# Score products of a block of heads: all over 128 rows first, then those over 64 rows with the halves of the rows in turn

## The chip, the core and the metric

The kernel runs on one core of a Trainium2 chip. The time is device microseconds (us) of one execution, as the median over several runs; lower is better. The program computes a whole small model (two different transformer stacks of two layers each, 256 tokens, model width 1024), with float32 inputs and outputs.

## The reference, cut to what matters

Three attentions of the second stack and one of the first make scores of queries and keys, add a bias or a mask, and take a softmax. Everything else (feed-forward products, experts, a recurrent time mix, output products) is not touched by the change.

```
# second stack, each of 2 layers; D = 64, S = 256
s = jnp.einsum('bhqd,bhkd->bhqk', q, k) * D ** -0.5        # neighbourhood, differential, window attention
p = softmax(s + bias)                                       # over the keys
o = jnp.einsum('bhqk,bkhd->bqhd', p, v)
# first stack, each of 2 layers: the same with a causal mask, for two branches (whole and selected keys)
```

## The kernel before, in words

TensorE (PE) multiplies operands that are split into two float32r parts, a high part and a low part: a product of two float32 numbers then has three terms (high by high, high by low, low by high). A head has 64 columns, so a score product contracts over 64 rows only. The kernel uses this: in a query tile `qs` the high part of a head stands in 64 of the 128 rows and its low part in the other 64; in the key tile `ks` the high part of the keys stands in both halves. One product over all 128 rows (`ks` by `qs`) therefore gives two of the three terms. The third (low part of the keys, `kl`, by the high part of the queries) is a product over the 64 rows of one half. `halves()` names the two halves of the rows: heads of half 0 have their high part in rows 0 to 63, heads of half 1 in rows 64 to 127.

So each head costs two PE products into the same columns of a PSUM bank: one over 128 rows, one over 64 rows. A block of heads takes two banks, one for heads of half 0 (`ps[0]`, `pS[0]`) and one for heads of half 1. `scores()` (lines 1989 to 1998, second stack) makes blocks of eight products, four heads with 256 keys each. `first()` inside `nsa()` (line 1247, first stack) makes blocks of sixteen products for the first 128 tokens (eight heads, 128 keys each) and of eight products for the second 128 tokens (four heads, 256 keys).

A pipeline of steps surrounds this: the scores of a block; then VectorE (DVE) adds the bias and takes the maximum of each head from the bank (line 1361), ScalarE (ACT) takes the exponentials (line 1363); the next block's scores; then PE transposes the first block's probabilities (line 1370) and multiplies them with the values. Between these steps stand pieces of "fill": big weight products (line 426, three passes high-high, low-high, high-low), whose weights arrive by DMA and are split by ACT (line 215) and DVE (line 216). In the first stack the fill also holds the small products of the recurrent mix, over 64 rows and 64 columns (lines 993 to 1150).

The program's order on each engine is fixed when it is built: a scheduler takes instructions out of the written order where its own estimate lets one run earlier. An engine carries out its own list in that order and waits on semaphores for the others.

Of the kernel before, what the change touches and what calls it, by code (L numbers as in the profile page):

```python
# [19 lines left out]
PSUM = bass.MemoryType.PSUM  # L20
# [15 lines left out]
# Big products run on operands that are split exactly into two float32r parts.  # L36
# [12 lines left out]
# A mix's streams are merged by these numbers of steps: time before the units and its fill; time, units and their fill;  # L49
# the last steps of time and the first half of the output product.  # L50
# [85 lines left out]
def _cols(w, at, n, step=512):  # L136
    """Column pieces of w from column at on."""
    return [w[:, c:c + min(step, at + n - c)] for c in range(at, at + n, step)]


def backwards(ap):
    """ap with its last dimension read from the end."""
    dims = [list(d) for d in ap.ap]
    step, n = dims[-1]
    dims[-1] = [-step, n]
    return bass.AP(tensor=ap.tensor, offset=ap.offset + step * (n - 1), ap=dims)


class Feed:
    """The weights in the order of their use, loaded and split into float32r parts ahead of the products."""  # L150
# [12 lines left out]
    def drop(self, phase):  # L163
        """The buffers of a phase go."""
        for kind in range(2):
            self.free[kind][:] = [s for s in self.free[kind] if s[0] != phase]
        assert self.part or not any(s[0] == phase for s in [r[1] for r in self.raws] + [s[1] for s in list(self.subs) + list(self.live)])

    def add(self, phase, srcs, split=True, heads=False):
        """srcs: DRAM [kb*128, n] in the order of their products; heads: columns (g j d) change to (j g d)."""  # L170
# [12 lines left out]
    def load(self):  # L183
        """Starts the next load, if a buffer is free."""
# [41 lines left out]
    def take(self, src):  # L226
        """The next row blocks of src: [(row block, part APs [128, n])]."""
# [6 lines left out]
    def done(self, n=1):  # L234
        """The products with the n oldest row blocks in hand are in the program."""
        for _ in range(n):
            self.free[1].append(self.live.popleft()[1])
# [11 lines left out]
class Operand:  # L249
    """Transposed parts [128, K, 256], put into the program by steps when products are about to need them."""  # L250
# [16 lines left out]
def merge(*streams):  # L267
    """The steps of all, each stream (steps, how many) kept as far along as the others."""
# [16 lines left out]
def weave(main, fill, ratio=1):  # L285
    """The steps of main with ratio steps of fill after each; what is left of fill stays."""
# [8 lines left out]
class Model:  # L295
# [75 lines left out]
    def banks(self, use):  # L371
        """The PSUM banks of a phase, by tag."""
        self.ps_use, self.ps_turn = use, {}
# [9 lines left out]
    def rows_to_columns(self, rows, name):  # L383
        """rows: list of (key, ap [r, 128]); returns a tile [128, R] and the first column of each key."""
# [25 lines left out]
    def put(self, parts, sel, src, scale=None):  # L410
        """parts[sel] = src * scale (scale: per-partition column or None)."""
# [10 lines left out]
    def mm(self, ps, lhs, rhs, start, stop):  # L422
        """lhs, rhs: lists of part APs."""
# [4 lines left out]
    def mul(self, xT, sub, targets, last):  # L428
        """targets: (ps, kind, at, opens, closes); kind 0: token tile at[0] of xT with the columns from at[1] on,
        1: the columns at(part) with xT, transposed; a bank has one that opens and one that closes it."""  # L430
# [10 lines left out]
    def products(self, xT, src, targets, evac, fine=False):  # L441
        """A step for each piece of the weights src; targets() -> as mul takes them; evac() at the end."""
# [17 lines left out]
    def tokens(self, xT, src, evac, banks=("lin", "lin"), tiles=(0, 1), fine=False):  # L460
        """evac(t, ps) with the products [128 tokens, n]."""
# [11 lines left out]
    def linear(self, xT, w, cols, evac, banks=("lin", "lin"), fine=False):  # L473
        """evac(t, c0, n, ps) for each chunk of columns; w: DRAM [K*128, N]."""
# [3 lines left out]
    def transposed(self, parts, src, nb, t, c0=0, k0=0, bank="tr"):  # L478
        """parts[:, k0+b, t*128:] = transposes of the nb column blocks of src [128, nb*128]."""
# [9 lines left out]
    def squares(self, h, ss):  # L489
        """ss[:, :, h] = the sums of squares of half of the columns of x."""  # L490
# [7 lines left out]
    def rstd(self, ss=None):  # L498
        """1/sqrt(mean(x^2) + eps) per token: [128, 2]."""
# [15 lines left out]
    def norm_T(self, gcol, pool=None):  # L515
        """Operand of (x*g) transposed, with rstd [128, 2]."""
# [19 lines left out]
    def start(self, gcol, pool=None):  # L536
        """The next phase's operand, as far as the first half of x's columns makes it."""
# [12 lines left out]
    def ffn(self, pool, xT, w1, w3, w2, done, tiles=(0, 1), hook=None):  # L550
        """Steps; done(t, c0, n, ps) takes the products; hook comes before the last of them."""
# [109 lines left out]
    def small_first(self, pool, l):  # L661
        """Loads the small weights of a layer of the first block."""
# [52 lines left out]
    def rope(self, pool, dst, src, t, heads):  # L715
        """dst, src: [128, heads, 64] of token tile t; the first 16 columns of each head."""
# [81 lines left out]
    def by_halves(self, ops, w, banks, hook=None, order=(0, 1), fine=False):  # L798
        """Steps: x += the products of two operands with the halves of the rows of w."""
# [17 lines left out]
    def mixed(self, l, pool, xT, src, zm, b0):  # L817
        """zm = the products transposed (blocks from b0 on), each token mixed with the one before it."""
# [56 lines left out]
    def head_norm(self, pool, src, eps, name, scratch, eng):  # L875
        """(src - mean) * rsqrt(var + eps) over the last of [128, nt, 4, 64], in scratch[0]."""
# [14 lines left out]
    def rwkv(self, l, pool, sw, zm, out):  # L891
# [5 lines left out]
        # normalised kk  # L897
# [12 lines left out]
        # decay and rates  # L910
# [70 lines left out]
        # products inside chunks of 64 tokens: [A^T | P^T | B^T | Q^T]  # L981
# [19 lines left out]
        # X = (I + A)^-1 by blocks of doubling size  # L1001
# [46 lines left out]
        # operands by token  # L1048
# [19 lines left out]
        # what does not need the state: U = -X B V and G = -X KK  # L1068
# [10 lines left out]
        # from chunk to chunk the state is S' = H^T S + C; the output is R^T S + Y  # L1079
# [38 lines left out]
        # bonus and gate  # L1118
# [39 lines left out]
    def compress(self, l, pool, sw, zk, out):  # L1158
        """out["cmp"]: the compressed keys [128, 32] and values [128, 8, 64], one block a head on the diagonal."""
# [56 lines left out]
    def nsa(self, l, pool, sw, qraw, zk, out):  # L1216
# [6 lines left out]
        # transposes  # L1223
# [23 lines left out]
        def first(t, br, j0):  # L1247
# [8 lines left out]
            for i in range(hb):  # L1256
                for gg, own, _ in self.halves():
                    q = qs[t][:, j0 + i, gg]
                    nc.tensor.matmul(pS[gg][:, i], q, ks[:, br, gg, 0:nk], start=True, stop=False)
                    nc.tensor.matmul(pS[gg][:, i], q[own], kl[own, br, 0:nk], start=False, stop=True)  # L1260
# [30 lines left out]
        # the compressed branch  # L1291
# [42 lines left out]
    def pipeline(self, pool, items, first, last, between=None, tag="tr"):  # L1334
        """Steps; each item's probabilities, their transposes and products, the next item's first ahead of the transposes."""
# [19 lines left out]
    def softmax_exp(self, pool, e, ps, bias, hb, sums, sink=None):  # L1355
        """e = exp(ps + bias - max), sums: its sums over the keys; returns -max; sink: minus what else the maximum takes in."""
# [23 lines left out]
    def ple_products(self, l, pT, pp, fine=False):  # L1380
        """pp [128, 2, 1024] = p @ ple_proj_w, by steps; pT: parts [128, 2, 256] of scratch."""
# [25 lines left out]
    def router(self, l, pool, temp):  # L1407
        """Loads the router's small weights."""
# [13 lines left out]
    def moe(self, l, wr, rb, sums, pp):  # L1422
        """Opens the buffers; yields what begins with the first half of x's columns and what does the rest."""
# [14 lines left out]
    def experts(self, l, pool, fp, ectx, km, gB, wr, rb, sums, pp):  # L1438
# [74 lines left out]
        # the tokens before each in its expert's list, and the lists' lengths  # L1513
# [33 lines left out]
    def dispatch(self, pool, e, off, km, sel, pos, tag, bufs):  # L1547
        """One-hot [128 tokens, 2, 128 slots]: slot off+c of expert e takes the token."""
# [7 lines left out]
    def expert_tokens(self, pool, e, km, sel, pos, gt, hs, got):  # L1556
        """got[e] = an expert's tokens transposed, their weights and 1/rms, and the way back; by steps."""
# [24 lines left out]
    def expert(self, pool, fp, tokens, w1, w3, w2, ahead):  # L1582
        """ahead: steps that make the next expert's tokens."""
# [18 lines left out]
    def expert_over(self, pool, e, km, sel, pos, gt, hs, w1, w3, w2):  # L1602
        """Slots 128 to 255 of an expert."""
# [55 lines left out]
    def row(self, pool, g):  # L1659
        """A vector [1024] in all partitions."""  # L1660
# [4 lines left out]
    def inner_norm(self, gB):  # L1665
        """x normalised, once the operand that is started has all of it; that gets both norms' 1/rms."""
# [8 lines left out]
    def outer_norm(self, pool, gB):  # L1675
        """x normalised, to the output."""
# [93 lines left out]
    def second_setup(self, pool, tp):  # L1770
        """Steps that make the tables of position biases."""
# [33 lines left out]
    def small_second(self, pool, l):  # L1805
        """Loads the small weights of a layer of the second block; w["steps"] makes the neighbourhood's biases."""
# [62 lines left out]
    def along(self, rstd, pool=None, bank="tr"):  # L1869
        """rstd [128, 2] per token -> [128, 256] with the tokens along the columns."""  # L1870
# [11 lines left out]
    def columns(self, xT, src, dst, scale, bank="lin", parts=None):  # L1882
        """dst [128, 256] of each block = the products transposed, by blocks of 128 columns, times rstd and scale;
        parts: what takes dst then."""
# [18 lines left out]
    # Scores are products over 64 rows: the parts of the queries stand above each other, the first part of the keys twice,  # L1903
    # so that one product has two of the three terms.
    def halves(self):
        return [(i, slice(i * 64, i * 64 + 64), slice(64 - i * 64, 128 - i * 64)) for i in range(2)]

    def queries(self, src, dst):
        """dst [128, blocks, 2, 256]: of each half of the rows its first part in place, its second in the other half's."""
# [5 lines left out]
    def keys(self, src, dst, low):  # L1915
        """dst [128, blocks, 2, 256]: of each half of the rows its first part in both halves; low: the second parts."""
# [6 lines left out]
    def attention(self, pool, l, xT, hook):  # L1923
# [14 lines left out]
        def query(c0, n=1):  # L1938
            """Steps and the queries of n times two blocks."""
# [20 lines left out]
        def pairs(q0, k0):  # L1960
            """Steps that make the queries and keys of four blocks, and they by twos."""
# [27 lines left out]
        def scores(qk, t, kb=lambda m: m):  # L1989
            """The scores of two heads of each half of the rows, in a bank each; kb(m): the block of head m's keys."""  # L1990
            qs, ks, kl = qk
            ps = [self.bank("sc").rearrange("p (h k) -> p h k", h=2) for _ in range(2)]
            for m in range(2):
                for i, own, _ in self.halves():
                    q = qs[:, m, i, t * P:(t + 1) * P]
# [233 lines left out]
```

## Time and profile before

| | |
|---|---|
| median of 3 runs | 2845.73 us (2842.85 to 2850.19) |
| span of the profiled execution (first to last instruction) | 2848.1 us |
| instructions in it | 38806 |
| busy share of the span: PE, DVE, ACT, POOL | 98%, 67%, 58%, 5% |
| mean granted PE clock | 0.976 of full speed |

The trace gives the profiled execution no time other than its span, which lies inside the range of the three runs, 2.4 us above their median. Busy time of PE counts an instruction from its start to its modelled end; two that overlap are not counted twice. The mean granted clock is 1 at 2.4 GHz and 0.5 at 1.2 GHz.

### The profile page before, as it was taken

The page shows a single profiled execution, that of the slowest core. Times are in us where ns is not written, and L with a number is a line of the kernel's source. Part 1 is how long each engine was busy: PE and PEld are TensorE (multiplying, and loading weights), DVE is VectorE, ACT ScalarE, POOL GpSimd, SP SyncE. Part 2 cuts the span into 40 slices and gives each one's busy share as a digit, 9 for nine tenths or more (in the row PEclk, how much of TensorE's full clock was granted, in tenths as well). Part 3 has the DMA queues.
Part 4 walks back from the last instruction along what each step waited for, and adds up shares of the span by engine and source line. Part 5 has one row for each costly group of instructions (what it writes and reads, how often), then busy time and mean ns, then how long its engine had stood idle before and what let it go on. Part 6 is the DMA issues. An engine that isn't in the chain of part 4 may idle for free. (4 is left out here: it accounts for less than half of the span.)

```text
span 2848.1 us, 38806 instructions
## 1 busy us (share of the span) xinstructions
PE 2794.6 (98%) x15206; PEld 2308.7 (81%) x15206; DVE 1911.7 (67%) x2586; ACT 1652.1 (58%) x2277; POOL 142.7 (5%) x183
## 2 busy tenths in 40 slices
PE   8999999999999999999989999999999999999998
PEld 7888887877888888888877888888888888888887
DVE  6446556547989989988886556666555556676554
ACT  6445456436777777777766445664444445664543
POOL 1220001320000000000000000010000000010000
PEclk9889999979999999999999999999999999999999
DMA  6208533307999999999975745444654546444651
GB/s 210 88 21 280 185 127 124 105 16 282 344 338 360 337 347 353 342 348 336 348 247 197 240 156 151 140 137 168 236 185 177 186 137 180 134 141 152 245 191 60
DMA packets 301542, 594.46 MB, mean 209 GB/s; under 512 B 25926, under 2 KB 78886, under 8 KB 301350
## 3 DMA queue, kind: packets, MB, share of 16 engines
q1 hardware_dynamic: 300102, 587.69, 59.8%
q0 software_dynamic: 1248, 4.20, 0.5%
q8 instruction: 122, 2.00, 0.3%
q14 instruction: 70, 0.57, 0.1%
HBM read 590.74 MB, written 1.10 MB: 208 GB/s over the span
## 5 line engine op out<-in xcount | busy, mean ns | idle before, releaser
L216 DVE TENSOR_TENSOR wl<-raw,wh 128x1024 fp32r<-128x1024 f32 (+1 forms) x1098 | 1316.2, 1219 | 605.7 <-ACT wh L215 594.4
L215 ACT ACTIVATE wh<-raw 128x1024 fp32r<-128x1024 f32 x1098 | 1136.8, 1049 | 767.1 <-PE ps L426 715.7
L426 PE MATMUL ps<-wh,xT 128*128 128x512 f32 (+2 forms) x2944 | 919.3, 388 | 11.8 <-ACT xT L419 3.7
L426 PEld LDWEIGHTS ps<-wh,xT 128*128 128x128 f32 x2944 | 544.2, 190 | 133.6 <-DVE xT L420 7.6
L426 PE MATMUL ps<-wl,xT 128*128 128x512 f32 (+2 forms) x1472 | 563.1, 383 | 0.5 <-DVE wl L216 0.5
L426 PE MATMUL ps<-wh,gT 128*128 128x512 f32 x1584 | 504.4, 391 | 0.0
L426 PE MATMUL ps<-wh,xe 128*128 128x512 f32 (+1 forms) x1536 | 458.6, 378 | 0.0
L426 PEld LDWEIGHTS ps<-wh,gT 128*128 128x128 f32 x1584 | 297.2, 188 | 62.0
L426 PEld LDWEIGHTS ps<-wh,xe 128*128 128x128 f32 x1536 | 279.2, 188 | 55.7
L426 PEld LDWEIGHTS ps<-wl,xT 128*128 128x128 f32 x1472 | 279.7, 190 | 53.6 <-DVE wl L216 2.0
L426 PE MATMUL ps<-wl,gT 128*128 128x512 f32 x792 | 309.5, 391 | 0.0
L426 PE MATMUL ps<-wl,xe 128*128 128x512 f32 (+1 forms) x768 | 289.4, 377 | 1.4 <-DVE wl L216 1.2
L426 PE MATMUL ps<-xT,wh 128*128 128x256 f32 x960 | 178.1, 287 | 5.7 <-ACT wh L215 2.9
L426 PEld LDWEIGHTS ps<-wl,gT 128*128 128x128 f32 x792 | 148.8, 188 | 30.9 <-DVE wl L216 0.5
L426 PEld LDWEIGHTS ps<-wl,xe 128*128 128x128 f32 x768 | 144.3, 188 | 32.3 <-DVE wl L216 5.0
L426 PEld LDWEIGHTS ps<-xT,wh 128*128 128x128 f32 x960 | 150.4, 193 | 8.0 <-ACT wh L215 3.1
L426 PE MATMUL ps<-xT,wl 128*128 128x256 f32 x480 | 135.9, 284 | 0.0
L1363 ACT ACTIVATE e<-e,mx 128x256 f32<-128x256 f32 (+1 forms) x160 | 76.1, 477 | 43.9 <-DVE mx L1361 43.5
L426 PEld LDWEIGHTS ps<-xT,wl 128*128 128x128 f32 x480 | 92.2, 193 | 0.3 <-DVE wl L216 0.3
L493 ACT ACTIVATE junk<-x 128x512 bf16<-128x512 f32 x56 | 35.2, 628 | 62.4 <-DVE x L547 47.8
L417 DVE TENSOR_TENSOR gT<-ps,gT 128x512 fp32r<-128x512 f32 (+1 forms) x108 | 66.5, 639 | 6.0 <-ACT gT L416 6.0
L416 ACT ACTIVATE gT<-ps 128x512 fp32r<-128x512 f32 (+1 forms) x108 | 56.9, 551 | 19.2 <-PE ps L485 19.0
(434 smaller groups left out, 2470.2 us busy)
## 6 DMA issues: line engine op xcount, KB each, us to landing
raw<-in_moe_w_dram SPq DMA_DIRECT2D x264, 1024.0 KB, 6.2
raw<-in_w_in_dram SPq DMA_DIRECT2D x50, 1024.0 KB, 5.4
raw<-in_ffn_w_gate_dram SPq DMA_DIRECT2D x44, 1024.0 KB, 5.1
raw<-in_ffn_w_up_dram SPq DMA_DIRECT2D x44, 1024.0 KB, 5.0
raw<-in_ffn_w_down_dram SPq DMA_DIRECT2D x44, 1024.0 KB, 5.5
raw<-in_ffn_w_dram SPq DMA_DIRECT2D x33, 1024.0 KB, 5.1
raw<-in_w_gate_dram SPq DMA_DIRECT2D x24, 1024.0 KB, 5.0
raw<-in_w_branch_dram SPq DMA_DIRECT2D x12, 1024.0 KB, 4.9
```

The costliest lines, as they stand in the source:

```text
L215: nc.scalar.activation(ho, w, AF.Copy)
L216: nc.vector.tensor_tensor(lw, w, ho.bitcast(F32), op=ALU.subtract)
L416: nc.scalar.activation(h, src, AF.Copy)
L417: nc.vector.tensor_tensor(l, src, hf, op=ALU.subtract)
L426: self.nc.tensor.matmul(ps, lhs[p], rhs[q], start=start and i == 0, stop=stop and i == last)
L493: self.nc.scalar.activation(junk, self.x[:, t, h * 512:(h + 1) * 512], AF.Square, accum_out=ss[:, t, h:h + 1])
L1363: nc.scalar.activation(e[:, i], e[:, i], AF.Exp, bias=mx[:, i:i + 1], scale=-1.0, accum_out=sums[:, i:i + 1])
```

## The change

A new function `score_products` takes the list of heads by pairs (one of each half of the rows) and writes all products over 128 rows first and then all over 64 rows, with half 0 and half 1 in turn. Both places that made scores call it. The number of products, their operands and their sizes stay as they are. The flag that opens a bank's accumulation is set at the bank's first product alone, and the one that closes it at its last. All other lines of the diff are comments and blank lines.

```
-            for i in range(hb):
-                for gg, own, _ in self.halves():
-                    q = qs[t][:, j0 + i, gg]
-                    nc.tensor.matmul(pS[gg][:, i], q, ks[:, br, gg, 0:nk], start=True, stop=False)
-                    nc.tensor.matmul(pS[gg][:, i], q[own], kl[own, br, 0:nk], start=False, stop=True)
+            self.score_products([[(pS[gg][:, i], qs[t][:, j0 + i, gg], ks[:, br, gg, 0:nk], kl[:, br, 0:nk]) for gg in range(2)]
+                                 for i in range(hb)])
...
+    def score_products(self, heads):
+        last = len(heads) - 1
+        for m, two in enumerate(heads):
+            for ps, q, ks, _ in two:
+                self.nc.tensor.matmul(ps, q, ks, start=m == 0, stop=False)
+        for m, two in enumerate(heads):
+            for (_, own, _), (ps, q, _, kl) in zip(self.halves(), two):
+                self.nc.tensor.matmul(ps, q[own], kl[own], start=False, stop=m == last)
...
-            for m in range(2):
-                for i, own, _ in self.halves():
-                    q = qs[:, m, i, t * P:(t + 1) * P]
-                    nc.tensor.matmul(ps[i][:, m], q, ks[:, kb(m), i], start=True, stop=False)
-                    nc.tensor.matmul(ps[i][:, m], q[own], kl[own, kb(m)], start=False, stop=True)
+            self.score_products([[(ps[i][:, m], qs[:, m, i, t * P:(t + 1) * P], ks[:, kb(m), i], kl[:, kb(m)]) for i in range(2)]
+                                 for m in range(2)])
```

The order on PE shows what the scheduler makes of it. First the second stack's first block of the first layer; rows with `ks` are products over 128 rows, rows with `kl` over 64 rows, `ps_19327` is the bank of half 0 and `ps_19328` that of half 1. Before:

```order
L426 MATMUL ps_19246<-xT_18858,wl_19175 128x256
L1996 MATMUL ps_19327<-ks_19018,qs_19017 128x256
L1997 MATMUL ps_19327<-kl_19019,qs_19017 128x256
L1996 MATMUL ps_19328<-ks_19018,qs_19017 128x256
L1997 MATMUL ps_19328<-kl_19019,qs_19017 128x256
L1996 MATMUL ps_19327<-ks_19018,qs_19017 128x256
L1997 MATMUL ps_19327<-kl_19019,qs_19017 128x256
L1996 MATMUL ps_19328<-ks_19018,qs_19017 128x256
L1997 MATMUL ps_19328<-kl_19019,qs_19017 128x256
L426 MATMUL ps_19356<-wh_19205,xT_18858 128x512
```

And the same place in the changed kernel:

```order
L426 MATMUL ps_19246<-xT_18858,wl_19175 128x256
L1911 MATMUL ps_19327<-ks_19018,qs_19017 128x256
L1911 MATMUL ps_19328<-ks_19018,qs_19017 128x256
L1911 MATMUL ps_19327<-ks_19018,qs_19017 128x256
L1911 MATMUL ps_19328<-ks_19018,qs_19017 128x256
L1914 MATMUL ps_19327<-kl_19019,qs_19017 128x256
L1914 MATMUL ps_19328<-kl_19019,qs_19017 128x256
L1914 MATMUL ps_19327<-kl_19019,qs_19017 128x256
L1914 MATMUL ps_19328<-kl_19019,qs_19017 128x256
L426 MATMUL ps_19356<-wh_19205,xT_18858 128x512
```

The eight products stand between the same two neighbours; the kind (128 or 64 rows) changes two times from there to the fill's next product, where it changed eight times.

Second, the first stack's first block of sixteen products (`ps_1387` and `ps_1388` are its two banks). Before, its first eight rows of sixteen:

```order
L1259 MATMUL ps_1387<-ks_1100,qs_1377 128x128
L1260 MATMUL ps_1387<-kl_1101,qs_1377 128x128
L1259 MATMUL ps_1387<-ks_1100,qs_1377 128x128
L1260 MATMUL ps_1387<-kl_1101,qs_1377 128x128
L1259 MATMUL ps_1387<-ks_1100,qs_1377 128x128
L1260 MATMUL ps_1387<-kl_1101,qs_1377 128x128
L1259 MATMUL ps_1388<-ks_1100,qs_1377 128x128
L1260 MATMUL ps_1388<-kl_1101,qs_1377 128x128
```

And the whole block in the changed kernel (x4 and x2 are so many in a row):

```order
L1911 MATMUL ps_1387<-ks_1100,qs_1377 128x128 x4
L1914 MATMUL ps_1387<-kl_1101,qs_1377 128x128 x2
L1911 MATMUL ps_1388<-ks_1100,qs_1377 128x128 x4
L1914 MATMUL ps_1388<-kl_1101,qs_1377 128x128 x2
L1914 MATMUL ps_1387<-kl_1101,qs_1377 128x128
L1914 MATMUL ps_1388<-kl_1101,qs_1377 128x128
L1914 MATMUL ps_1387<-kl_1101,qs_1377 128x128
L1914 MATMUL ps_1388<-kl_1101,qs_1377 128x128
L426 MATMUL ps_1369<-wh_1234,xT_125 128x512
```

Here the scheduler does not keep the written order: four of the second bank's products over 128 rows stand behind two of the first bank's over 64 rows, so the kind changes four times instead of sixteen, and products of one half stand next to each other.

Counted over the whole order on PE, changes of kind into or out of a score product over 64 rows go from 192 to 52 in the second stack (24 blocks), from 60 to 14 in the first stack's blocks with 128 keys, and from 64 to 30 in its blocks with 256 keys. In the second stack nothing else on PE moves by more than a few places. In the first stack the small products of the mix, the transposes of probabilities and a few weight products change places with the score products, and on DVE and ACT some instructions of the softmax, of the mix and of the weight splits stand a few places earlier or later (86 rows of difference on DVE, 35 on ACT, none on SP's queue of loads).

## Rows read from the trace of the kernel before

**Rows 1.** The page's first part: busy time, share of the span, instructions.

```profile
PE 2794.6 (98%) x15206; PEld 2308.7 (81%) x15206; DVE 1911.7 (67%) x2586; ACT 1652.1 (58%) x2277; POOL 142.7 (5%) x183
```

**Rows 2.** Windows: busy PE, PEld, DVE, ACT, POOL; then PE clock, DMA share, GB/s.

```profile
2480.00:2540.00 60.00, 60.00 (x347) 49.73 (x346) 47.51 (x111) 43.30 (x87) 8.67 (x7) 1.00 0.39 126
```

**Rows 3.** Who PE waited for: the longest total (us, times, longest).

```profile
PE ps L525 <- PEq L1543: 5.4, 1, 5.4
```

**Rows 4.** Groups of PE instructions by form: rows of contraction, shape, count | busy, mean ns.

```profile
L1997 PE MATMUL ps<-kl,qs 64*128 64x256 f32 x96 | 36.6, 381 | 0.0
...
L1260 PE MATMUL ps<-kl,qs 64*128 64x256 f32 x32 | 14.0, 437 | 0.0
...
L1260 PE MATMUL ps<-kl,qs 64*128 64x128 f32 x32 | 12.5, 421 | 0.0
```

**Rows 5.** Timeline of PE in the second stack's first block: start, duration, instruction.

```profile
1755.57 0.28 PE L426 MATMUL ps<-xT,wl 128*128 128x256 f32 x1
...
1755.91 0.28 PE L426 MATMUL ps<-xT,wl 128*128 128x256 f32 x1
...
1756.70 0.28 PE L1996 MATMUL ps<-ks,qs 128*128 128x256 f32 x1
1756.91 0.38 PE L1997 MATMUL ps<-kl,qs 64*128 64x256 f32 x1
1757.22 0.38 PE L1996 MATMUL ps<-ks,qs 128*128 128x256 f32 x1
...
1759.10 0.50 PE L426 MATMUL ps<-wh,xT 128*128 128x512 f32 x1
```

**Rows 6.** Timeline of PE, mix: 64-row products, L915 on rows 0-63, L918 on 64-127.

```profile
47.23 0.48 PE L915 MATMUL ps<-tw,waup 64*128 64x256 f32 x1
47.24 0.48 PE L918 MATMUL ps<-zm,waup 64*128 64x256 f32 x1
47.55 0.38 PE L915 MATMUL ps<-tw,waup 64*128 64x256 f32 x1
...
47.76 0.38 PE L915 MATMUL ps<-tw,waup 64*128 64x256 f32 x1
```

**Rows 7.** Windows, as in Rows 2, of the first stack's stretches at the lower clock.

```profile
131.00:133.90 2.90, 2.90 (x9) 2.08 (x8) 0.66 (x7) 0.33 (x2) 0.00 (x0) 0.60 0.00 0
...
182.00:202.00 20.00, 19.94 (x174) 17.14 (x175) 7.05 (x19) 3.72 (x11) 7.40 (x6) 0.52 0.00 1
558.50:570.00 11.50, 11.50 (x55) 8.77 (x56) 3.09 (x26) 5.43 (x25) 0.00 (x0) 0.50 0.01 1
590.00:626.00 36.00, 36.00 (x190) 29.90 (x188) 11.00 (x37) 9.31 (x31) 7.78 (x6) 0.50 0.00 1
```

**Rows 8.** Timeline of PE in the first stack's two blocks with 128 keys, layer 0.

```profile
129.07 0.22 PE L1259 MATMUL ps<-ks,qs 128*128 128x128 f32 x1
...
129.48 0.33 PE L1259 MATMUL ps<-ks,qs 128*128 128x128 f32 x1
129.73 0.32 PE L1260 MATMUL ps<-kl,qs 64*128 64x128 f32 x1
...
133.53 0.47 PE L1260 MATMUL ps<-kl,qs 64*128 64x128 f32 x1
133.94 1.22 PE L426 MATMUL ps<-wh,xT 128*128 128x512 f32 x2
...
135.81 0.31 PE L1259 MATMUL ps<-ks,qs 128*128 128x128 f32 x1
...
141.50 1.97 PE L1033 MATMUL ps<-X,am 64*64 64x64 f32 x32
```

**Rows 9.** Timeline around a softmax of the second stack: DVE, ACT, PE's weight load.

```profile
1885.28 0.48 DVE L1361 CUSTOM_DVE_ANT_0 e<-ps,T,nsink 128x256 f32<-128x256 f32 x1 [0.96 <-PE ps L1997]
...
1887.30 0.49 ACT L1363 ACTIVATE e<-e,mx 128x256 f32<-128x256 f32 x1
...
1888.46 0.59 PEld L1370 LDWEIGHTS ps<-ident,e 128*128 128x128 f32 x4
```

## The prediction

> **What bounds the kernel now.** I began with the busy shares: PE is busy 98% of the span, DVE 67%, ACT 58% [rows 1]. Then the waits of PE: the largest in total is 5.4 us, at the program's start [rows 3], so PE is the bound nearly everywhere, and time goes where PE's own instructions take it. That holds where the scores are made: in a window of the second stack's attention PE is busy 60.00 of 60 us, DVE 47.51, ACT 43.30, the loads 0.39 of the queues' time [rows 2]. So PE time saved there is saved in the end, as long as DVE, the next busiest at 79%, keeps up.
>
> A busy PE need not be a PE that multiplies, so I looked at starts, not durations. In the second stack's first block the product over 128 rows starts at 1756.70, the one over 64 rows at 1756.91, the next over 128 rows at 1757.22, and the product behind the block at 1759.10 [rows 5]: from the second product on one every (1759.10 - 1756.91) / 7 = 0.313 us. Weight products of the same 256 columns, all over 128 rows, stand just ahead in the same rows: from 1755.57 to 1755.91 three of them start, 0.113 us each. Each change of kind, from 128 to 64 rows or back, thus costs 0.313 - 0.113 = 0.20 us. The trace shows neither wait nor idle for it; it lies inside "busy".
>
> **What removing it gives: the second stack.** Its 96 products over 64 rows [rows 4] stand in 24 blocks of 8 products. A block now lasts 1759.10 - 1756.70 = 2.40 us. After the change I place the starts as follows, from the block's first start:
> - four products over 128 rows at 0, 0.11, 0.23, 0.34;
> - the first over 64 rows 0.21 later, as now after a product over 128 rows [rows 5]: 0.55;
> - whether the two halves run side by side the attention doesn't show, since two products over 64 rows never follow each other in it. The mix has the nearest rows: a product over rows 0 to 63 starts at 47.23, the one over rows 64 to 127 at 47.24, and so on by pairs [rows 6]. They are other products (float32 in passes of 0.21 us), but of the same two kinds of rows and into two banks. So I take pairs: the second product over 64 rows starts with the first;
> - the second pair: in the mix a first product over 64 rows holds up the next on its rows for 0.32 us, later ones for 0.21 [rows 6]; the extra 0.11 is the weight load that nothing hides after a change. Here that is 0.11 + 0.11 = 0.22 us: 0.77;
> - the next product over 128 rows: 0.313 less the 0.11 of the load, which the first pair has hidden: 0.98.
>
> That saves 2.40 - 0.98 = 1.42 us a block and 34.1 us for 24. By the order 52 changes of kind remain, not 48, as transposes split two blocks; 4 x 0.20 = 0.8 us less: **33 us**. Bounds of the part that the attention doesn't show: without pairs the four start at 0.55, 0.77, 0.88, 0.99 and the block ends at 1.20 (28 us in all, with the 0.8 off); with a load that is never hidden on 64 rows either it ends at 1.41 (23 us).
>
> A load could also stay unhidden among products over 128 rows; but the three weight products in 0.34 us [rows 5] do have their loads hidden, though each uses all rows, and I go by that. The Trainium skill ("TensorE: Matmul & The Clock Gate", part 3, what overlaps and what doesn't) has a rule against it: a weight load overlaps a running product only where it goes to another group of rows. By it a block would end at 1.30 and the second stack would give 26 us; the rows of this trace do not bear it out for products over 128 rows, and no row shows it for two halves of float32r.
>
> **The first stack, blocks with 128 keys** (64 products in two layers: 32 over 64 rows [rows 4] and as many over 128). In layer 0 the two blocks of sixteen take 133.94 - 129.07 = 4.87 and 141.50 - 135.81 = 5.69 us [rows 8]; I take layer 1 as equal: 21.1 us. At full clock the spacing is 0.25 us (129.48 to 129.73). Without a change of kind I put it at 0.11, the weight load, as with 256 columns; so a change costs 0.14 to 0.15 us here. Inside these blocks the granted clock falls: it is 0.60 of full speed from 131.0 to 133.9 and 0.50 from 558.5 to 570 [rows 7], that is the level of 1.2 GHz, and the spacing goes to 0.41 us (133.53 to 133.94). What PE did before was this chain of changes alone.
>
> After the change 14 changes of kind are left of 60: 64 x 0.11 + 14 x 0.15 = 9.1 us at full clock, 12 saved. If the clock stays up, the weight products between and behind the blocks (133.94 to 135.81, and some 3.5 us behind 141.50, in both layers) run at full speed as well, 10.8 us at half clock being 5.4 saved: 17 together. If the clock falls all the same, the blocks take up to twice 9.1 us and 3 are saved. I lean to the clock staying up, since the blocks shrink to some 2.3 us and stand between weight products, and take **14 us**, the difference to 17 being new waits: the softmax must now be read from the bank (DVE) before the second block may write it, in less time.
>
> **Blocks with 256 keys** (64 products, 32 over 64 rows [rows 4]): 64 changes become 30; 34 x 0.20 = 6.8 us, up to 1.7 more for those in the stretch from 590 to 626 at half clock [rows 7]; less some waits, **6 us**. The low stretches 182 to 202 and 590 to 626 [rows 7] hold mostly small products of the mix, transposes and value products, and I leave them as they are; were the second to get its clock back, 18 us more would be saved.
>
> **Waits that could come.** Both banks of a block now end together, so DVE's first maximum comes nearer to the block's end. In the block that starts at 1883.40 the first maximum starts at 1885.28, 1.88 us later; after the change the seventh product closes that bank and DVE starts at about 0.77 + 0.42 = 1.19. DVE and ACT are thus 0.69 us earlier, PE 1.42: the chain loses 0.73 us to PE. Its slack: ACT's last exponential ends at 1887.30 + 0.49 = 1887.79, and PE loads the first of the transposes at 1888.46 [rows 9]: 0.67 us. But the first four transposes need only the first bank's exponentials, 1 us earlier. So the wait is 0 to 0.1 us a block, up to 2 us. Moved instructions of the mix in the first stack may add as much; for both I take off 4 us.
>
> **Sum:** 33 + 14 + 6 - 4 = 49 us. The span of 2848.1 lies 2.4 us over the median of the runs, 2845.7, within their spread; I take the saving off the median: **2797 us**.
>
> **Rivals.**
> - *Half of it (0.20).* The pairs run one after the other, and the clock falls in the first stack all the same: 28 + 3 + 5 - 3 = 33 us, 2813. For it: in the first stack the scheduler often puts products of one half behind each other, and rows of pairs exist for float32 alone. Against it: the starts in [rows 6].
> - *The price belongs to each product over 64 rows, not to the change (0.06).* Then each keeps 0.313 us: the block ends at 0.34 + 0.21 + 4 x 0.313 = 1.80, 0.6 saved x 24 = 14, and some 8 in the first stack: 2824. Against it: 0.21 from 47.55 to 47.76 for a pair [rows 6].
> - *No load hidden behind a product on the same rows (0.03).* Then products over 128 rows stand 0.11 + 0.11 apart: 0, 0.22, 0.44, 0.66; the pairs at 0.87 and 1.09, the end at 1.30: 1.10 saved x 24 - 0.8 = 26 us, with 14 + 6 - 4 as above 42: 2804. The weight products of [rows 5] speak against it. (It is the skill's rule above.)
> - *No change (0.03)*: PE gains, and DVE and ACT, whose softmax comes as late as now, take it back in waits at the transposes: 2846. For it: slack of only 0.67 us; against it: the first maximum also moves up.
> - *Slower (0.03)*: the spacing stays at 0.313 us whatever the order. Then the first bank closes with the seventh product instead of the sixth, and every softmax starts 0.31 us later: with 24 blocks and 16 in the first stack 12 us, 2858, if no slack absorbs it. It decides only where PE gets less than 0.31 us a block out of the order; the weight products' 0.113 us speak against that.
>
> My own case, 0.65, is the likeliest: **2797 us**. Range: down to 2780 (pairs, no new waits, the clock up around the blocks with 128 keys, and part of the stretch from 590 back at full clock: 33 + 17 + 8 + 8 = 66), up to 2820 (the first rival without the pairs' or the loads' gain: 23 in the second stack, 3 in the first). Left out are the price per product, no change and slower, 0.12 together. Less than 0.3% (8.5 us) is about what a measurement of this kernel can't tell from no change. Faster by more: 0.65 + 0.20 + 0.06 + 0.03 = 0.94; within: 0.03; slower: 0.03.
>
> **What would show it.** Right: in the second stack a block lasts about 1 us, `kl` products start by pairs, the distance of two products over 128 rows is 0.11 us; the granted clock is 1 around the first stack's blocks with 128 keys; PE's waits stay small. Wrong: `kl` products 0.11 or 0.3 us apart; new waits of PE for ACT's exponentials or DVE's maxima in the waits' view; low-clock stretches longer than now, or moved rather than gone.

## The result, and the profile after

The changed kernel takes **2768.44 us** (median of 4 runs, 2764.87 to 2771.73), the kernel before beside it 2845.47 us (4 runs, 2842.85 to 2850.19): a ratio of 0.9726, 95% interval 0.9709 to 0.9743. That is 77 us less, where 49 were forecast, and the time lies under the forecast range (2780 to 2820). The profiled execution has a span of 2765.4 us, 82.7 less than the profiled one of before.

The page's first part of the changed kernel:

```profile
PE 2709.7 (98%) x15206; PEld 2257.8 (82%) x15206; DVE 1909.0 (69%) x2586; ACT 1648.7 (60%) x2277; POOL 141.9 (5%) x183
```

PE is still busy 98% with as many instructions; its busy time alone fell by 84.9 us [rows 1]. Timeline of PE in the second stack's first block, and the weight product behind a later block (in brackets the idle time ahead of it, and for what it waited):

```profile
1703.13 0.63 PE L1911 MATMUL ps<-ks,qs 128*128 128x256 f32 x4
1703.69 0.50 PE L1914 MATMUL ps<-kl,qs 64*128 64x256 f32 x4
1704.13 0.50 PE L426 MATMUL ps<-wh,xT 128*128 128x512 f32 x1
...
1816.08 0.50 PE L426 MATMUL ps<-wh,xT 128*128 128x512 f32 x1 [0.77 <-DVE merged L2033]
```

The four products over 128 rows take 0.56 us, the four over 64 rows 0.44: the block lasts 1704.13 - 1703.13 = 1.00 us, against 2.40 [rows 5]. Summed over the same timeline, from each block's first product to what follows it, all 24 blocks take 28.1 us instead of 57.3. Six of them last 1.27 to 1.91 us instead of 1.00, some 3.5 us in all. Three of the six hold a new wait, 2.2 us together: 1.6 for DVE's sum of the branches (`merged`; the last row shows one half of it) and 0.6 for a maximum of DVE. The other three are 0.3 us longer each, and no wait is recorded there.

Timeline of PE around the blocks with 128 keys in the first stack's layer 0, to the first transposes of probabilities, then the first score product and the same transposes of layer 1; behind it these transposes, and both marks of layer 1, in before:

```profile
128.77 0.56 PE L1911 MATMUL ps<-ks,qs 128*128 128x128 f32 x4
129.26 0.43 PE L1914 MATMUL ps<-kl,qs 64*128 64x128 f32 x2
130.13 0.63 PE L1911 MATMUL ps<-ks,qs 128*128 128x128 f32 x4 [0.43 <-DVE qs L1921]
...
137.26 0.60 PE L1367 MATMUL ps<-ident,e 128*128 128x128 f32 x4
...
533.68 0.66 PE L1911 MATMUL ps<-ks,qs 128*128 128x128 f32 x4
...
540.14 0.60 PE L1367 MATMUL ps<-ident,e 128*128 128x128 f32 x4
```

```profile
145.72 0.60 PE L1370 MATMUL ps<-ident,e 128*128 128x128 f32 x4
...
555.22 0.33 PE L1259 MATMUL ps<-ks,qs 128*128 128x128 f32 x1
...
570.58 1.05 PE L1370 MATMUL ps<-ident,e 128*128 128x128 f32 x4
```

From the first score product to these transposes it is 137.26 - 128.77 = 8.49 us, and was 145.72 - 129.07 = 16.65 [rows 8]: 8.2 us less. The same two marks in layer 1 (533.68 and 540.14, before 555.22 and 570.58) are 8.9 us nearer to each other. Between the marks stand the same PE instructions before and after, 74 in layer 0 and 68 in layer 1, so the two sum to 17.1 us for the blocks with 128 keys and what stands close behind them.

Where the rest came from shows in a mark between the stacks, the first activation of the mixture of experts. One line's instructions, before and then after: engine, count, shortest/median/longest in ns, first and last start in us.

```profile
L592 ACT ACTIVATE sa<-ps,gs x48: 454/690/696, 692.8 to 1474.3; 128x512 f32<-128x512 f32 x40, 128x256 f32<-128x256 f32 x8
```

```profile
L592 ACT ACTIVATE sa<-ps,gs x48: 454/689/696, 640.3 to 1421.5; 128x512 f32<-128x512 f32 x40, 128x256 f32<-128x256 f32 x8
```

The first stack ends 692.8 - 640.3 = 52.5 us earlier, all behind it adds 82.7 - 52.5 = 30.2. Forecast were 20 for the first stack and 33 for the second, less 4. So the surprise lies in the first stack, and behind its blocks with 128 keys: 52.5 - 17.1 = 35.4 us where 6 were forecast. Four windows of it, before and then after, columns as in [rows 2] (the last but two is the granted clock), and the two later stretches of before by themselves:

```profile
120.00:160.00 40.00, 39.91 (x271) 29.63 (x270) 19.97 (x68) 18.17 (x55) 4.00 (x4) 0.83 0.16 53
160.00:230.00 70.00, 68.98 (x533) 56.43 (x533) 40.68 (x96) 34.61 (x69) 12.94 (x10) 0.85 0.24 83
530.00:580.00 50.00, 49.90 (x507) 38.43 (x506) 24.33 (x73) 25.94 (x62) 8.13 (x15) 0.86 0.19 64
580.00:640.00 60.00, 59.19 (x438) 47.85 (x437) 24.75 (x75) 18.45 (x51) 15.01 (x12) 0.69 0.00 1
...
182.00:204.00 22.00, 21.94 (x190) 18.86 (x189) 7.34 (x20) 4.78 (x13) 7.73 (x6) 0.53 0.00 1
588.00:628.00 40.00, 40.00 (x217) 32.71 (x216) 11.78 (x41) 10.62 (x36) 7.78 (x6) 0.53 0.00 1
```

```profile
120.00:160.00 40.00, 39.46 (x356) 31.59 (x355) 24.27 (x79) 25.99 (x72) 7.18 (x5) 1.00 0.22 75
160.00:230.00 70.00, 68.58 (x544) 56.35 (x543) 46.94 (x102) 39.55 (x72) 10.49 (x9) 1.00 0.48 175
530.00:580.00 50.00, 48.80 (x526) 40.74 (x525) 31.49 (x111) 30.87 (x91) 12.88 (x10) 1.00 0.10 35
580.00:640.00 60.00, 55.91 (x340) 41.89 (x339) 42.97 (x98) 29.42 (x48) 4.36 (x4) 0.97 0.62 222
```

The clock is full nearly throughout. In before the two later stretches ran at a mean of 0.53: if all their time went with the clock, the same work would have taken 22 x 0.47 + 40 x 0.47 = 29.1 us less at full speed. That estimate is from above: in layer 0 it gives 10.3 us, and equal instructions in experiment 7 show 8.6. So most of the 35.4 us is the clock; what the blocks with 256 keys gave by themselves, and a change of order in layer 1, come with experiments 7 and 8.

Two theories stood before the runs. **A:** the price is the change between 128 and 64 rows, and chains of such changes also bring the clock down, so that the small products behind them run at half speed. **Rivals:** the halves of the rows in turn are what helps; or the later low stretches come from the small products themselves or by chance, and only the changes' own price went.

### The profile page after: what moved, and what is told of

Its sections match the earlier page's. It is cut to its first block, busy times and chain, and to the rows that moved or that the text cites. A ratio compares the mean times of both kernels' runs of the same rounds, so it can differ in the third digit from the quotient of the medians.

```text
span 2765.4 us, 38810 instructions
## 1 busy us (share of the span) xinstructions
PE 2709.7 (98%) x15206; PEld 2257.8 (82%) x15206; DVE 1909.0 (69%) x2586; ACT 1648.7 (60%) x2277; POOL 141.9 (5%) x183
```

## The experiments

Each was timed beside the kernel before on the same chip: 2844.82 us beside 1, 2, 3 and 5 (13 runs), 2844.71 beside 4, 6, 7 and 8 (9 runs), 2847.28 beside 9 (13 runs). Single executions of before lay between 2824.21 and 2853.00 us, at mean granted clocks of 0.987 to 0.975, which suggests that not every execution has all the falls. In the diffs, `score_products` has a switch, and without it writes the products as before: `(heads, False)`.

**1. The new order in the second stack alone (e1_second_only), and 2. in the first alone (e2_first_only).** In 1 the call in the first stack has the switch, in 2 that in the second:

```diff
-                                 for i in range(hb)])
+                                 for i in range(hb)], False)
```

> The new order in the second stack's 24 blocks alone; the first stack keeps the old one, product by product. Theory A (the second stack gives its 1.4 us a block, the rest of the 77 us comes out of the first stack, most of it as clock): 30 us under the kernel before, about 2815; the four low-clock stretches of the first stack's score part stay as they were before (about 85 us at half clock). Rival B (the clock or the order elsewhere owes something to the second stack's change, or the runs before had a low clock by chance): 2800 or less, with fewer low-clock stretches in the first stack.

> The new order in the first stack's blocks alone; the second stack keeps the old one. Theory A: 50 us under the kernel before, about 2795, no low clock between the first score product and the output product of each layer of the first stack; blocks of the second stack at 2.4 us. Rival C (the first stack gives only its own switches, about 17 + 5 us, and the rest of the 77 us lies in the second stack or in chance): about 2823.

Measured: 2817.73 us for the second stack alone (ratio 0.9909, 0.9879 to 0.9938), 27 less; 2798.73 us for the first alone (0.9847, 0.9791 to 0.9904), 46 less. The two sum to 73 of the 77. The larger part of the gain is the first stack's, which makes two thirds as many of these products and was forecast at 20 against 33. Windows of its stretches, with the new order in the second stack alone and then in the first alone:

```profile
182.00:204.00 22.00, 21.93 (x191) 18.85 (x189) 7.33 (x20) 4.79 (x12) 7.72 (x6) 0.53 0.00 1
588.00:628.00 40.00, 40.00 (x214) 33.13 (x214) 11.57 (x40) 9.83 (x32) 7.76 (x6) 0.51 0.00 1
```

```profile
130.00:146.00 16.00, 15.56 (x118) 12.57 (x118) 7.42 (x40) 8.19 (x35) 0.00 (x0) 0.68 0.19 67
182.00:204.00 22.00, 21.06 (x188) 17.34 (x185) 14.84 (x35) 7.59 (x13) 4.57 (x4) 1.00 0.16 50
588.00:628.00 40.00, 36.01 (x189) 24.85 (x188) 29.91 (x60) 18.90 (x34) 3.65 (x4) 0.96 0.63 217
```

The low stretches go with the first stack's order. A shorter fall, between 130 and 146, still appears in the second of these profiles (0.68): the new order does not exclude one there. Of the six profiles with the new order in the blocks with 128 keys, two show a fall of over 4 us around these blocks (2 and 3); of the three with the old order of changes (before, 1 and 8) all do.

**3. The halves of the rows apart (e3_halves_apart):** all products over the first half of the rows, then all over the second, instead of in turn.

```diff
-        for m, two in enumerate(heads):
-            for (_, own, _), (ps, q, _, kl) in zip(self.halves(), two):
-                self.nc.tensor.matmul(ps, q[own], kl[own], start=False, stop=m == last)
+        (_, lo, _), (_, hi, _) = self.halves()
+        for m, ((p0, q0, _, l0), _) in enumerate(heads):
+            self.nc.tensor.matmul(p0, q0[lo], l0[lo], start=False, stop=m == last)
+        for m, (_, (p1, q1, _, l1)) in enumerate(heads):
+            self.nc.tensor.matmul(p1, q1[hi], l1[hi], start=False, stop=m == last)
```

> As the changed kernel, but within the products over 64 rows first all of half 0, then all of half 1, each on a line of its own. If halves in turn run side by side and that is worth a product: a block of the second stack lasts 1.1 us instead of 1.0, in all 3 to 6 us more than the changed kernel (2772 to 2775). If only the number of changes of kind counts: the same block and the same time as the changed kernel within 2 us.

**4. The changed kernel with a line for each half (e0_lines)**, otherwise the same, timed later, to see the halves apart in the trace.

> The changed kernel with the products over the two halves of the rows on a line each, otherwise the same. All theories: 2768 us. If the halves run side by side, the two lines show the same starts within 0.02 us, pair after pair, as with the halves written apart; if they run one after the other, the second line starts behind the first by one product's own time.

Measured: 2773.09 us with the halves apart (0.9758, 0.9703 to 0.9814), 2765.76 with a line for each (0.9734, 0.9706 to 0.9762). Timeline of PE in the second stack's first block, first of the halves apart (L1920 the first half, L1922 the second), then of a line for each (L1920 and L1921):

```profile
1713.75 0.63 PE L1917 MATMUL ps<-ks,qs 128*128 128x256 f32 x4
1714.31 0.38 PE L1920 MATMUL ps<-kl,qs 64*128 64x256 f32 x1
1714.32 0.38 PE L1922 MATMUL ps<-kl,qs 64*128 64x256 f32 x1
1714.53 0.28 PE L1920 MATMUL ps<-kl,qs 64*128 64x256 f32 x1
...
1714.75 0.50 PE L426 MATMUL ps<-wh,xT 128*128 128x512 f32 x1
```

```profile
1700.64 0.63 PE L1917 MATMUL ps<-ks,qs 128*128 128x256 f32 x4
1701.20 0.38 PE L1920 MATMUL ps<-kl,qs 64*128 64x256 f32 x1
1701.20 0.38 PE L1921 MATMUL ps<-kl,qs 64*128 64x256 f32 x1
...
1701.63 0.50 PE L426 MATMUL ps<-wh,xT 128*128 128x512 f32 x1
```

The halves run side by side in both, and the block lasts 1.00 us in both. So "in turn", half of what the change says, does nothing in a block of the second stack. Neither expectation for 3 holds whole: the block is the same, but the median lies 5 to 7 us over those of the changed kernel and of 4. In the profiles the longer time lies in the first stack: the first activation of the mixture of experts starts at 653.1 us with the halves apart and at 639.7 in 4. With the halves apart the clock is at half from about 540 to 546 and from 563 to 574 us, in 4 at neither place; whether this order brings the falls wasn't tried. That profile, of an execution of 2779.50 us, also shows that a later fall is not excluded by the new order.

**5 and 6. No change of kind at all, in the order of before (e4_full_rows, and again e8_full_rows_again beside the changed kernel):** the third product runs over all 128 rows. The sums then carry one more small term, the low part of the query times the low part of the other half's keys. Against before, the second stack's product (the first stack's is changed in the same way):

```diff
-                    nc.tensor.matmul(ps[i][:, m], q[own], kl[own, kb(m)], start=False, stop=True)
+                    nc.tensor.matmul(ps[i][:, m], q, kl[:, kb(m)], start=False, stop=True)
```

> The kernel before with its old order, but the third product taken over all 128 rows too (query and low key parts of both halves): each score gets, beside its three terms, the product of two low parts, of its query and of the other half's head's key. No change of kind is left, nothing else is added. If the price is that of changing between 128 and 64 rows: eight products 0.11 us apart, a block of the second stack 0.9 us, the first stack at full clock, 3 to 8 us under the changed kernel, 2760 to 2766. If the price lies in the old order itself (two products in a row into the same columns, or another weight each time): 0.31 us apart as before and about 2845.

> The order of before, the third product over all 128 rows (it adds a small term of the other half's head), again, timed beside the changed kernel. Theory A (the price is the change between 64 and 128 rows): as fast as the changed kernel or a few us faster, 2760 to 2768 us, no stretch of half clock in the first stack's scores. Rival (the order counts by itself): slower than the changed kernel by more than 10 us.

Measured: 2763.14 us (0.9727, 0.9672 to 0.9782), and again 2760.95 (0.9708, 0.9682 to 0.9734; 2758.35 to 2762.07) beside 2765.76 for the changed kernel (2763.78 to 2772.16). Of the second, the timeline of PE in the second stack's first block, and a window of the first stack that had the longest fall (in the other three of its windows the granted clock is 1.00 too):

```profile
1701.54 0.28 PE L1996 MATMUL ps<-ks,qs 128*128 128x256 f32 x1
1701.66 0.28 PE L1997 MATMUL ps<-kl,qs 128*128 128x256 f32 x1
...
1702.50 0.40 PE L426 MATMUL ps<-wh,xT 128*128 128x512 f32 x1
```

```profile
580.00:640.00 60.00, 55.99 (x380) 43.13 (x374) 44.14 (x104) 29.28 (x49) 4.37 (x4) 1.00 0.61 222
```

With before's own order, 0.12 us from product to product and 0.96 us a block. The price was never the order, it was the change between 128 and 64 rows; and without it none of the four low stretches comes either, with all small products of the mix still there. PE's order around the scores of the first stack is that of before in both layers: 600 instructions in a row from the mix's products at 127.42 us take 56.03 us instead of 76.93, and 699 from 552.82 take 78.27 instead of 107.63. Products over 64 rows by themselves don't bring the falls: the changed kernel has as many, with fewer changes, and in its profile the four falls are gone but for some 3 us at 612.

This version is some 5 us faster than the changed kernel, every run below every run of the other. In the profiles of 6 and 4 it gains nothing up to the first activation of the mixture of experts (640.9 us against 639.7); the 24 blocks of the second stack sum to 26.5 us against 28.3, which explains 1.8 us, and the rest stays open.

**7. The new order only in the blocks with 128 keys (e5_128keys_only), and 8. only in those with 256 keys (e6_256keys_only),** both in the first stack, the second stack as before. In 7 (in 8 with `t == 1`):

```diff
-                                 for i in range(hb)])
+                                 for i in range(hb)], t == 0)
```

> The new order only in the first stack's blocks with 128 keys; those with 256 keys and the second stack keep the old one. Theory A (a chain of products that change between 128 and 64 rows brings the clock down, and the small products behind it keep it there): the stretches of half clock at 130 to 146 and 558 to 572 us go, those at 182 to 204 and 589 to 627 stay, about 17 us less than before, 2828 us. Rival B (the later falls are only a sequel of the first ones): all four go, about 46 us less, 2799 us. Rival C (chance of the run): the falls stand as before, only the changes themselves go, about 9 us less, 2836 us.

> The new order only in the first stack's blocks with 256 keys. Theory A: the stretches of half clock at 182 to 204 and 589 to 627 us go, those at 130 to 146 and 558 to 572 stay; 46 us of the whole first stack less the 17 of its blocks with 128 keys, about 29 us less than before, 2816 us. Rival B (the later falls are a sequel of the first ones): they stay, and only the changes of kind go, about 6 us less, 2839 us. Rival D (the later falls come from the small products alone, whatever stands ahead of them): they stay too, 2839 us.

Measured: 2802.18 us for the blocks with 128 keys (0.9863, 0.983 to 0.9895), 42.5 less; 2812.85 for those with 256 keys (0.9894, 0.9862 to 0.9925), 31.9 less. The first is nearest to rival B, the second to theory A; neither holds both. Windows of the first stack, first of 7, then of 8:

```profile
120.00:160.00 40.00, 39.47 (x345) 30.69 (x345) 24.41 (x80) 24.33 (x67) 7.19 (x5) 1.00 0.18 57
160.00:230.00 70.00, 68.76 (x535) 55.49 (x534) 45.28 (x99) 39.20 (x75) 11.34 (x9) 1.00 0.47 172
530.00:580.00 50.00, 49.27 (x464) 38.56 (x461) 30.43 (x105) 29.63 (x88) 12.85 (x10) 0.98 0.13 43
580.00:640.00 60.00, 56.36 (x407) 43.67 (x407) 42.30 (x106) 26.75 (x49) 4.36 (x4) 0.99 0.58 204
```

```profile
120.00:160.00 40.00, 39.91 (x286) 30.38 (x286) 21.12 (x72) 20.13 (x62) 5.01 (x4) 0.87 0.17 54
160.00:230.00 70.00, 68.58 (x582) 56.73 (x582) 47.69 (x106) 41.10 (x79) 12.69 (x10) 1.00 0.45 163
530.00:580.00 50.00, 49.22 (x392) 37.83 (x391) 29.01 (x88) 25.75 (x71) 9.09 (x7) 0.86 0.13 43
580.00:640.00 60.00, 56.11 (x442) 43.60 (x441) 40.50 (x101) 27.23 (x58) 9.11 (x8) 1.00 0.40 144
```

In 8 the early falls stay (0.87 and 0.86) and the later ones are gone. In 7 all are gone but for some 3 us at 578, though the blocks with 256 keys are written as before. So a later fall of 20 or 38 us took both: the chain in the blocks with 256 keys, and something of the blocks with 128 keys ahead of it. Taking either away saves most of what the later falls cost; the gains of 42.5 and 31.9 sum to 74.4 where both together give 46.1, so some 28 are in both.

For 8 the comparison is clean: PE's order is that of before in both layers, but for the products inside the blocks. For 7 it is clean in layer 0 alone. In layer 1 the scheduler gave PE another order of blocks and small products in 7, and the same one in 9 and in the changed kernel, so there the first chain is not the only thing that differs from before.

How equal the work of layer 0 was can be seen in the timeline of PE from the first product of the blocks with 256 keys on, in before and then in 7:

```profile
154.94 0.36 PE L1259 MATMUL ps<-ks,qs 128*128 128x256 f32 x1
...
182.72 0.60 PE L1370 MATMUL ps<-ident,e 128*128 128x128 f32 x2
...
203.34 0.39 PE L869 MATMUL ps<-gv,ws 128*128 128x128 f32 x2
```

```profile
146.70 0.36 PE L1912 MATMUL ps<-ks,qs 128*128 128x256 f32 x1
...
174.48 0.39 PE L1367 MATMUL ps<-ident,e 128*128 128x128 f32 x2
...
186.53 0.39 PE L869 MATMUL ps<-gv,ws 128*128 128x128 f32 x2
```

For 182.72 - 154.94 = 27.78 us the two run alike, 8.24 us apart; then the same two transposes take 0.60 us in before and 0.39 in 7. At the last row, 404 instructions behind the first and in the same order, the distance is 16.81 us: the fall cost 8.6 us. What stood ahead decided, or the place in time.

**9. The same as 7, moved (e9_later):**

```diff
+            if (t, br, j0) == (0, 0, 0):
+                for _ in range(70):
+                    nc.tensor.matmul(pS[0][:, 0], qs[t][:, j0, 0], ks[:, br, 0, 0:nk], start=True, stop=True)
```

> As with the new order in the blocks with 128 keys alone, and in each layer of the first stack 70 more products over 128 rows (128 by 128) ahead of the first of these blocks, which are overwritten and leave the result as it is. At 0.12 us each they move all that follows by 8.3 us, so that the old-order blocks with 256 keys of the first layer begin at 155 us, where those of before began (154.94). Theory S (the second fall of a layer needs the first one ahead of it): no stretch of half clock behind them, 2802 and twice 8.3, 2819 us. Rival T (the second fall goes by where in time the blocks stand, whatever the clock did ahead of them): half clock behind them again for some 20 and 38 us, half of that as loss, 2847 us; in between, about 2828 to 2838, if in one layer alone.

Measured: 2822.39 us (10 runs, 2813.11 to 2835.48), close to theory S (2819) and far from rival T (2847). Its first stack's windows:

```profile
160.00:230.00 70.00, 68.75 (x571) 55.49 (x570) 46.40 (x107) 38.92 (x77) 13.52 (x10) 1.00 0.39 137
...
580.00:640.00 60.00, 56.24 (x456) 43.68 (x452) 35.53 (x89) 22.97 (x50) 11.08 (x9) 0.91 0.29 101
```

In layer 0 there is no fall, with the blocks with 256 keys beginning at 153.49 us, near the 154.94 of before. In layer 1, whose order on PE is that of 7, the profile has one short fall, from about 591 to 598 us, right behind the old-order blocks with 256 keys: such a chain can bring the clock down without an earlier fall, but here for 7 us, not for 38, and the runs' spread of 22 us suggests that it does so in some executions only. The test of the place in time is thus that of layer 0.

## Why the prediction was wrong, and where it was right

- **PE is the bound, and PE time saved is saved in the end:** right. PE is at 98% before and after, and the 84.9 us of busy time that it lost came out as 82.7 us of span.
- **A block of 0.98 us in the second stack:** right; 1.00, with 0.56 to the first product over 64 rows (placed at 0.55) and 0.22 from pair to pair. The pairs taken from the mix hold for these products too. The second stack gave 29.2 us by its blocks, 30.2 by the marks, 27 alone, for 33 less its waits.
- **4 us of new waits:** the size about right, the place wrong, so the number is partly luck. I looked for them where the transposes wait for the exponentials; in the second stack PE shows no such wait, but 2.2 us for `merged` and a maximum, in blocks that are 3.5 us longer in all.
- **Blocks with 128 keys:** the mechanism right, the size short: 17.1 us, the sum before I took 3 off for waits of the second block. The profile shows one wait there, of 0.43 us ahead of the product at 130.13, and it is for the queries (`qs`), not for a bank.
- **Blocks with 256 keys, 6 us:** right. Summed from each block's first product to what follows it, they take 19.5 us in the profile of 7, in the old order at full clock, and 12.6 in the changed kernel: 6.9 us for 34 changes, 0.20 each. The medians of 7 and 2 lie 2802.18 - 2798.73 = 3.5 us apart, which from two sets of runs tells little.
- **The step that failed** is "The low stretches 182 to 202 and 590 to 626 [rows 7] hold mostly small products of the mix, transposes and value products, and I leave them as they are". I put the cause of a low clock into what ran inside the stretch. The runs show it ahead of the stretch: the same small products ran at full clock, but for at most 3.4 us, in seven profiles (the changed kernel, 2, and 4 to 8) in which one of the chains ahead was shorter or had no change of kind. By the marks 35.4 us went behind the blocks with 128 keys where 6 were forecast: 29 of the 33.7 us by which the profiled pair's 82.7 passes the forecast of 49. Of the 35.4, 6.9 are the changes' own price in the blocks with 256 keys; the other 28.5 are the clock and, in layer 1, the new order on PE, which are not separated here. The range took in 8 of the 18 us that I priced for the second stretch, and nothing for the first.
- **Rivals:** "Half of it" fell with the pairs and the clock. "The price belongs to each product over 64 rows" fell with four of them in 0.44 us. "No load hidden behind a product on the same rows" fell with 0.12 us from product to product over 128 rows in experiment 6; by it they would stand 0.22 apart. "No change" fell with waits of a few us only, and "slower", a spacing that stays at 0.313 us, with the block of 1.00.

Open stays what exactly about a chain of changes lowers the clock, why a second fall lasted 20 and 38 us only behind a first one, what the other order in layer 1 does to the clock, why 3 has falls in layer 1, and some 3 of the 5 us between the changed kernel and the one over full rows.

## What to carry to other kernels

Where products over 64 and over 128 rows alternate, look at the distance of their starts, not at PE's busy share: sorting them into runs of one kind, or giving all of them the full rows (where the result may carry the extra term), takes away a price that no wait shows. And when a stretch runs at the lower clock, look for the cause in what PE did ahead of it as well as in what it does inside: a forecast that shortens such work should price every low stretch behind it as a case of its own, and expect gains of two edits to overlap when each alone removes the same stretch.

## What the runs showed of the hardware

- A change between products over 128 and 64 rows costs 0.20 us at 256 columns and 0.14 to 0.15 at 128, inside PE's busy time: 2.40 us a block with seven changes, 1.00 with one inside it, 0.96 with none. The Trainium skill ("TensorEngine Tiling (Array Packing)", Key Properties under Tiling Modes) says that changing the tiling mode drains TensorE. The trace agrees that such a change costs time, at these prices; the drain itself it does not show.
- Products on different halves of the rows need not stand next to each other to run side by side: with the halves apart, the third product over 64 rows in PE's order (the first on the other half) starts at 1714.32, 0.21 us ahead of the second at 1714.53. The Trainium skill ("TensorE: Matmul & The Clock Gate", Part 3, what overlaps and what doesn't) has matmuls start strictly in program order; the records of this run do not agree for two groups of rows.
- The granted clock fell to 0.50, the level of 1.2 GHz, while PE was busy by its records (40.00 of 40 us from 588 to 628 in before). It fell behind chains of products that change between 128 and 64 rows; with the same order and no change none of the four falls came (experiments 5 and 6). In layer 0 two chains worked together: the same 404 instructions had a fall of some 20 us behind a first chain of changes (before) and none without it (7). In layer 1 the second chain was followed by 38 us at the lower level in before, by 3 in 7 and 7 in 9, where PE's order differed too.
